# The order of the matmuls in a block product: the low half of the weights last

## The chip, the cores and the metric

The kernel runs on one core of a Trainium2 chip. The metric is the device time of one execution in microseconds (us), the median over several runs. Five engines matter. TensorE multiplies (PE in the profile; its loads of the stationary operand are the rows called PEld). VectorE (DVE) and ScalarE (ACT) do elementwise work, GpSimd (POOL) issues some transfers and a few elementwise operations, and SyncE (SP) issues the other transfers. Each engine takes its instructions in the order in which the program gives them, and waits where an operand is not ready yet.

## The reference, cut to what matters

The model is a two-layer encoder over 512 tokens of width 1024 (layer 0 mixes tokens by attention, layer 1 by a gated linear recurrence). Behind each mixer stands a multilayer perceptron, and only these two perceptrons are touched:

```python
D_MODEL, SEQ, DEPTH = 1024, 512, 2
D_FF = 4 * D_MODEL

def squared_relu_mlp(h, w1, w2):
    u = jax.nn.relu(h @ w1)
    return (u * u) @ w2

h = rms_norm(x, norm_mlp[layer])
x = x + squared_relu_mlp(h, mlp_w1[layer], mlp_w2[layer])
```

All of it is in 32-bit floats. The upward matrix `w1` is 1024 by 4096, the downward matrix `w2` 4096 by 1024.

## The kernel before, in words

**Halves.** The operands of these matmuls are tiles of the type fp32r. To keep the accuracy, each operand is split into a high half (the value cast to that type, names that end in `h`) and a low half (the rest, names that end in `l`), and a product is three matmuls: high by high, high by low, low by high. The split of a block of weights is two instructions of 128x1024 elements: ScalarE casts the raw block to `wh`, and then VectorE subtracts, `wl = raw - wh` (function `operand`). The activations are split in the same way, into `xgh`/`xgl` (the perceptron's input), and `bh`/`bl` and `sh`/`sl` (the squared hidden values).

**Quarters and block products.** The 4096 hidden features are worked through in four quarters (0 to 3). In each quarter the kernel computes hidden features from the input (the upward part) and multiplies them into the output (the downward part). Both parts use a scheme of Strassen's kind: seven block products, P1 to P7, on sums of blocks, take the place of eight. A quarter therefore has 14 upward steps (two halves p = 0 and 1 of the quarter, each in the order P1 P5 P6 P3 P7 P2 P4) and 14 downward steps. The downward steps are in a written order, `ORDERS["mid"]`: P1 0, P5 0, P1 1, P2 0, P5 1, P6 0, P6 1, P3 0, P3 1, P7 0, P7 1, P2 1, P4 0, P4 1, where the digit is the half g of the quarter. The last quarter of layer 1 has its own order, `"last"`, in which P2 1 stands behind P5 1. Quarter 0 has no upward steps here (plain products made it before). `run` lists all steps of a layer and goes through them; the last two downward steps of a layer (P4 0 and P4 1) are run by a function `end` and call `times`.

**An upward step** (`up`, matmuls on L976) is 24 matmuls of 256 columns: for two output halves i and four k, `wh` by h, `wl` by h, `wh` by l. The weights are the stationary operand. All 24 go into one bank of PSUM.

**A downward step** (`part` and `times`, matmuls on L1071) is 12 matmuls of 512 columns: for two token blocks i and two feature blocks j, h by `wh`, h by `wl`, l by `wh`. Here the activations are the stationary operand. Each i has a PSUM bank of its own. P1, P6, P7 and P4 go on adding to the same pair of banks (called X, `ps_t` in the trace), P5 and P3 to the pair V (`ps_acc`), P2 has the pair W (`ps_z`). Behind each step with g = 1, `collect` adds both banks to the output sums `c`, by one VectorE instruction a bank.

**What sets the order.** TensorE's order is the program's. Within a perceptron VectorE's and ScalarE's are too: the class `Ordered` chains each of their instructions behind the one before, so they all carry its line, L765. `leave(i)` issues what follows step i: copies out of PSUM, collects, and by `prepare(i + 4)` the additions of weight blocks, the split of hidden values that are still waiting (`split_slot`) and the split of the weights of the step four later (`make`, `operand`). There are four buffers for `wh` and four for `wl`, so the cast of step i + 4 takes the buffer of step i and cannot start before the last matmul that reads it. Transfers that add one block of weights to another in memory are issued from GpSimd (L1053).

Of the kernel before, what the change touches and what calls it, by code (L numbers as in the profile page):

```python
# [17 lines left out]
P = 128  # L18
S = 512
D = 1024  # L20
C = D // P
# [40 lines left out]
def hybrid_encoder(  # L62
# [24 lines left out]
    V, A, G, PE = nc.vector, nc.scalar, nc.gpsimd, nc.tensor  # L87
# [212 lines left out]
    with ExitStack() as actx:  # L300
# [12 lines left out]
        for i in range(2):  # L313
            both = []
            for nm in ("h", "l"):
                t = sp.tile([P, 2 * P], F32R, tag=f"last{nm}{i}", name=f"last{nm}{i}")
# [10 lines left out]
        q, kh, kl, v, w = {}, {}, {}, {}, {}  # L327
# [72 lines left out]
        sums = hp.tile([P, S], F32, tag="early", name="ssq")  # L400
# [4 lines left out]
        with tc.manual_schedule(engines=others):  # L405
# [26 lines left out]
            for k in range(C):  # L432
                for n, (low, y) in enumerate(((0, xgh), (0, xgl), (1, xgh))):
                    for i in range(2):
                        PE.matmul(
                            first[i], parts[i][low][:, k, :], y[:, k, :], start=k == n == 0,
                            stop=k == C - 1 and n == 2,
# [261 lines left out]
        steps = chain(*(g for g, _ in fill))  # L699
# [53 lines left out]
    HS = S // 2  # L753
# [21 lines left out]
    class Mlp:  # L775
# [191 lines left out]
        def up(self, name, w, ps, new):  # L967

            block = self.PRODUCTS[name][0]
            w = [t.rearrange("p j (k n) -> p (j k) n", n=2 * P) for t in w]  # L970
            for i in range(2):
                for k in range(C // 2):
                    h, l = self.xa(block, k)
                    wh, wl = (t[:, k, i * P : (i + 1) * P] for t in w)
                    for n, (m, y) in enumerate(((wh, h), (wl, h), (wh, l))):
                        PE.matmul(  # L976
                            ps[:, i * HS : (i + 1) * HS], m, y,
                            start=new and i == k == n == 0,
                            stop=i == 1 and k == C // 2 - 1 and n == 2,
                            skip_group_check=not new,  # L980
                        )

# [112 lines left out]
        def part(self, sums, name, g, w):  # L1097

            to = self.PRODUCTS[name][3]
            if to not in sums:  # L1100
                sums[to] = [self.bank() for _ in range(2)]
            for i in range(2):
                self.times(name, g, i, w, sums[to][i], name in ("P1", "P5", "P2"))

        OPEN_AT = 36
        UP = "P1", "P5", "P6", "P3", "P7", "P2", "P4"
# [297 lines left out]
    with ExitStack() as rctx:  # L1404
# [35 lines left out]
        ps, xc, aa, a0, om, z, gin, pg = ({} for _ in range(8))  # L1440
# [161 lines left out]
        for k in range(C):  # L1602
            for c in range(4):
                ps, wh, wl = begun[c]
# [196 lines left out]
```

## Time and profile before

| | |
|---|---|
| time, median of 3 runs | 1035.65 us (1035.09 to 1036.73) |
| the profiled execution's own time | 1035.46 us |
| its span | 1033.7 us |
| PE, PEld busy | 1023.5 us (99%), 890.9 us (86%) |
| DVE, ACT, POOL busy | 859.0 us (83%), 701.7 us (68%), 170.9 us (17%) |
| granted clock of TensorE | 0.999 |
| perceptron of layer 0, downward part of quarter 0 to the last step | about 290 to 563 us |
| perceptron of layer 1, the same | about 755 us to the end |

A row of the timeline gives the start in us from the beginning of the span, the duration in us, the engine, the line, the operation, output and inputs by the program's names, the shape, and in brackets the engine's idle time just before, with what ended it. Matmuls overlap one another and their ends are modelled, so the time that a matmul takes from the array is read from the distance between the starts of two of them, and not from its duration. A row of a group ends with the busy time, the mean of one in ns, and the idle time before the group's instructions.

### The profile page before, as it was taken

How to read it: one execution, taken by the hardware profiler on the slowest of the kernel's cores; microseconds unless marked ns; L12 is line 12 of the kernel's file. 1: busy time of each engine (PE TensorE's matmuls, PEld its weight loads, DVE VectorE, ACT ScalarE, POOL GpSimd, SP SyncE). 2: the span in 40 equal slices, each digit the busy share in tenths (PEclk: the TensorE clock that was granted, in tenths of full speed). 3: DMA queues.
4: the chain of work that ended last, by engine and by line, in shares of the span. 5: the costliest groups of instructions: out<-in, count | busy, mean ns of one | idle time of the engine just before them, and what ended most of it. 6: DMA issues, size and time to landing. Idle time of an engine off the chain costs nothing.

```text
span 1033.7 us, 15863 instructions
## 1 busy us (share of the span) xinstructions
PE 1023.5 (99%) x5862; PEld 890.9 (86%) x5862; DVE 859.0 (83%) x1148; ACT 701.7 (68%) x1083; POOL 170.9 (17%) x239
## 2 busy tenths in 40 slices
PE   9999999999999999999999999999999999999997
PEld 7888888888888988988988888888888988988986
DVE  6888787848788898898899888984789898898897
ACT  6777676836766873873875799964755773873866
POOL 0444344420010010010011121200010010010013
PEclk9999999999999999999999999999999999999999
DMA  7745354527536767667682575452436767667653
GB/s 241 212 121 144 114 151 103 159 97 288 145 77 190 183 139 201 172 139 200 173 207 79 153 185 151 103 223 83 101 66 182 180 146 194 171 145 198 165 117 111
DMA packets 53260, 160.46 MB, mean 155 GB/s; under 512 B 6720, under 2 KB 8256, under 8 KB 53184
## 3 DMA queue, kind: packets, MB, share of 16 engines
q1 hardware_dynamic: 42096, 120.35, 35.7%
q0 software_dynamic: 10656, 38.80, 22.6%
q8 instruction: 46, 0.75, 0.3%
q10 hardware_dynamic: 432, 0.31, 0.1%
q14 instruction: 30, 0.25, 0.1%
HBM read 137.41 MB, written 4.19 MB: 137 GB/s over the span
## 4 chain that ended last, share of the span: by engine, by line
PE 76%; DVE 12%; ACT 7%; issue 3%; DMA 1%; DVEq 0%; ACTq 0%; POOL 0%; POOLq 0%
PE ps_t L1071 10%; PE ps_acc L976 7%; DVE wl L765 5%; PE ps_acc L229 5%; PE ps_acc L231 5%; PE ps_acc L230 5%; PE ps_acc L1071 5%; PE ps_z L976 3%; ACT wh L765 3%; ACT u L765 3%; PE ps_t L229 2%; PE ps_z L1071 2%; PE ps_t L231 2%; PE ps_t L230 2%; DVE b L765 2%
## 5 line engine op out<-in xcount | busy, mean ns | idle before, releaser
L765 ACT CAST wh<-b 128x1024 fp32r<-128x1024 f32 x168 | 174.8, 1050 | 124.2 <-DVE b L765 79.2
L765 DVE TENSOR_TENSOR wl<-b,wh 128x1024 fp32r<-128x1024 f32 x168 | 203.5, 1219 | 43.3 <-ACT wh L765 42.8
L1053 POOL DMA_DIRECT2D b<-in_w_dn x40 | 35.0, 874 | 362.7 <-DVE b L765 268.3
L229 PE MATMUL ps_acc<-xgh,wh 128*128 128x512 f32 x192 | 78.5, 409 | 0.0
L231 PE MATMUL ps_acc<-xgl,wh 128*128 128x512 f32 x192 | 75.2, 392 | 0.0
L230 PE MATMUL ps_acc<-xgh,wl 128*128 128x512 f32 x192 | 75.1, 391 | 0.0
L224 DVE TENSOR_TENSOR wl<-raw,wh 128x512 fp32r<-128x512 f32 (+2 forms) x70 | 62.1, 914 | 14.5 <-ACT wh L222 14.3
L589 DVE TENSOR_TENSOR_SCAN scan<-keep,later 128x128 f32<-128x128 f32 (+1 forms) x64 | 59.5, 933 | 17.5 <-ACT keep L579 12.0
L765 ACT ACTIVATE u<-u 128x512 f32<-128x512 f32 x100 | 63.1, 632 | 9.8 <-DVE u L765 8.2
L222 ACT CAST wh<-raw 128x512 fp32r<-128x512 f32 (+2 forms) x70 | 50.7, 759 | 20.4 <-PE ps_acc L231 7.3
L593 POOL TENSOR_TENSOR w<-w,scan 128x128 f32<-128x128 f32 (+1 forms) x64 | 51.7, 810 | 58.4 <-DVE scan L589 56.4
L1053 POOL DMA_DIRECT2D b<-in_w_up x24 | 20.8, 868 | 236.6 <-DVE b L765 69.1
L765 DVE TENSOR_TENSOR b<-b,b 128x1024 f32<-128x1024 f32 x48 | 58.7, 1222 | 1.3
L765 DVE TENSOR_TENSOR u<-u 128x512 f32<-128x512 f32 (+1 forms) x92 | 54.8, 596 | 3.1 <-ACT u L765 1.1
L765 ACT CAST wh<-raw 128x1024 fp32r<-128x1024 f32 x46 | 48.1, 1048 | 8.4 <-PE ps_acc L1071 8.3
L976 PE MATMUL ps_z<-xgh,wh 128*128 128x256 f32 x192 | 53.1, 277 | 0.1
L976 PE MATMUL ps_z<-xgh,wl 128*128 128x256 f32 x192 | 53.0, 276 | 0.0
L976 PE MATMUL ps_acc<-low,wh 128*128 128x256 f32 x192 | 53.0, 276 | 0.0
L1071 PE MATMUL ps_t<-wl,sh 128*128 128x512 f32 x126 | 49.7, 395 | 1.1 <-DVE wl L765 1.1
L1071 PE MATMUL ps_t<-wh,sl 128*128 128x512 f32 x126 | 49.7, 394 | 0.0
L1071 PE MATMUL ps_t<-wh,bh 128*128 128x512 f32 x126 | 49.2, 390 | 0.0
L1071 PE MATMUL ps_t<-wh,sh 128*128 128x512 f32 x126 | 49.1, 390 | 0.0
(399 smaller groups left out, 3408.7 us busy)
## 6 DMA issues: line engine op xcount, KB each, us to landing
b<-in_w_dn SPq DMA_DIRECT2D x48, 512.0 KB, 4.4
b<-in_w_dn POOLq DMA_DIRECT2D x40, 512.0 KB, 5.7
b<-in_w_up SPq DMA_DIRECT2D x36, 512.0 KB, 4.8
b<-in_w_up POOLq DMA_DIRECT2D x24, 512.0 KB, 5.6
raw<-in_w_m SPq DMA_DIRECT2D x16, 512.0 KB, 4.5
raw<-in_w_dn SPq DMA_DIRECT2D x16, 512.0 KB, 4.6
raw<-in_w_in SPq DMA_DIRECT2D x16, 512.0 KB, 3.8
raw<-in_w_qk SPq DMA_DIRECT2D x12, 512.0 KB, 3.7
```

What stands on the lines that cost most here:

```text
L222: A.copy(wh[:, k, :], raw[:, k, :])
L224: V.tensor_tensor(wl[:, k, :], raw[:, k, :], f(wh[:, k, :]), ALU.subtract)
L229: PE.matmul(ps, wh, ah, start=start, stop=False)
L230: PE.matmul(ps, wl, ah, start=False, stop=False)
L231: PE.matmul(ps, wh, al, start=False, stop=stop)
L589: V.tensor_tensor_scan(sc[:, S - n : S][:, ::-1], keep[:, :n][:, ::-1], later[:, S - n :][:, ::-1], 1.0, ALU.mult, ALU.max,)
L593: G.tensor_tensor(wt, wt, sc[:, S - n + 1 : S + 1], ALU.mult)
L765: ins = getattr(self.e, name)(*args, **kwargs)
L976: PE.matmul(ps[:, i * HS : (i + 1) * HS], m, y, start=new and i == k == n == 0, stop=i == 1 and k == C // 2 - 1 and n == 2, skip_group_che ...
L1053: G.dma_start(out=unit[b].rearrange("p j n -> p (j n)"), in_=unit["src"](to), accum_op=ALU.add)
L1071: PE.matmul(ps, m, y[:, jj, cols], start=first and n == 0, stop=last and n == 2, skip_group_check=not new,)
```

## The change

The order of the matmuls within a step changes, in the upward and in the downward steps. Neither their number nor their operands change. In an upward step, first come the 16 matmuls with `wh` (h and l by turns, through both i and all k), and then the eight with `wl`. In a downward step, first come the eight with `wh` (h and l by turns, through i and j), and then the four with `wl`. The flags that open and close the sums in PSUM move to the first and the last matmul of the new order. `part` now has the loop itself; `times` is left as it was, for `end`.

```diff
 # up
-            for i in range(2):
-                for k in range(C // 2):
-                    h, l = self.xa(block, k)
-                    wh, wl = (t[:, k, i * P : (i + 1) * P] for t in w)
-                    for n, (m, y) in enumerate(((wh, h), (wl, h), (wh, l))):
-                        PE.matmul(
-                            ps[:, i * HS : (i + 1) * HS], m, y,
-                            start=new and i == k == n == 0,
-                            stop=i == 1 and k == C // 2 - 1 and n == 2,
-                            skip_group_check=not new,
-                        )
+            steps = [(low, i, k) for low in range(2) for i in range(2) for k in range(C // 2)]
+            for low, i, k in steps:
+                h, l = self.xa(block, k)
+                wh, wl = (t[:, k, i * P : (i + 1) * P] for t in w)
+                for m, y in ((wl, h),) if low else ((wh, h), (wh, l)):
+                    PE.matmul(
+                        ps[:, i * HS : (i + 1) * HS], m, y,
+                        start=new and i == k == low == 0 and y is h,
+                        stop=(low, i, k) == steps[-1], skip_group_check=not new,
+                    )
 # part
-            for i in range(2):
-                self.times(name, g, i, w, sums[to][i], name in ("P1", "P5", "P2"))
+            block, new = self.PRODUCTS[name][0], name in ("P1", "P5", "P2")
+            wh, wl = w
+            steps = [(low, i, j) for low in range(2) for i in range(2) for j in range(2)]
+            for low, i, j in steps:
+                h, l = (t[:, j, block, i * P : (i + 1) * P] for t in self.a[g])
+                for m, y in ((h, wl),) if low else ((h, wh), (l, wh)):
+                    PE.matmul(
+                        sums[to][i], m, y[:, j, :],
+                        start=new and g == j == low == 0 and m is h,
+                        stop=g == low == j == 1, skip_group_check=not new,
+                    )
```

## The prediction

> **What bounds the kernel now.** I read the page first, then the groups of PE and PEld by shape, then the timeline of PE alone in one downward part, and then VectorE's and ScalarE's rows beside it.
>
> ```profile
> PE 1023.5 (99%) x5862; PEld 890.9 (86%) x5862; DVE 859.0 (83%) x1148; ACT 701.7 (68%) x1083; POOL 170.9 (17%) x239
> L1071 PEld LDWEIGHTS ps_t<-wl,sh 128*128 128x128 f32 x126 | 23.6, 188 | 8.3 <-DVE wl L765 3.5
> ```
>
> PE is the bound, and by its 99% it seems to have nothing to give. The second row says otherwise: loads that go with a matmul on `wl` wait for VectorE. The modelled ends hide it, so I take starts. This is the downward part of layer 0, quarter 2: the first matmuls of P1 1, P2 0, P5 1, P6 0, P6 1 (with its second and third) and P3 0.
>
> ```profile
> 450.04 0.39 PE L1071 MATMUL ps_t<-wh,sh 128*128 128x512 f32 x1
> ...
> 452.87 0.39 PE L1071 MATMUL ps_z<-wh,bh 128*128 128x512 f32 x1
> ...
> 455.83 0.39 PE L1071 MATMUL ps_acc<-wh,sh 128*128 128x512 f32 x1
> ...
> 458.81 0.39 PE L1071 MATMUL ps_t<-wh,bh 128*128 128x512 f32 x1
> ...
> 461.53 0.39 PE L1071 MATMUL ps_t<-wh,sh 128*128 128x512 f32 x1
> 462.13 0.50 PE L1071 MATMUL ps_t<-wl,sh 128*128 128x512 f32 x1 [0.21 <-DVE wl L765]
> 462.47 0.40 PE L1071 MATMUL ps_t<-wh,sl 128*128 128x512 f32 x1
> ...
> 464.80 0.39 PE L1071 MATMUL ps_acc<-wh,bh 128*128 128x512 f32 x1
> ```
>
> ```profile
> 449.73 0.69 DVE L765 TENSOR_TENSOR sl<-u,sh 128x512 fp32r<-128x512 f32 x1
> 460.85 1.23 DVE L765 TENSOR_TENSOR wl<-b,wh 128x1024 fp32r<-128x1024 f32 x1 [0.57 <-ACT wh L765]
> 463.13 0.74 DVE L765 SCALAR_TENSOR_TENSOR c<-ps_acc,rr,c 128x512 f32<-128x512 f32 x1
> ```
>
> A step without a wait, P6 0, takes 461.53 - 458.81 = 2.72 us, 0.227 a matmul. P2 0 takes 2.96, P5 1 2.98 and P6 1 3.27: 0.24, 0.26 and 0.55 lost, 1.05 a quarter. In P6 1 the cause can be read. The second matmul should start at 461.53 + 0.227 = 461.76, but VectorE ends `wl` at 460.85 + 1.23 = 462.08. It starts 0.05 later, at 462.13, and the third comes 0.34 behind it in place of 0.227: a late operand costs its lateness, plus 0.05, plus 0.11 for the load that could not be made ahead, 0.165 together. P1 1 loses 0.11 in another way: `sl` ends at 449.73 + 0.69 = 450.42, while the third matmul, the first to read it, is due at 450.04 + 2 x 0.227 = 450.49; less than 0.165 ahead, so about 0.1 is lost.
>
> The Trainium skill ("TensorE: Matmul & The Clock Gate", "Step-by-step: what each phase is for") says that TensorE pulls weight loads ahead of running matmuls. In a downward product the load is of h and not of `wl`, so by that rule nothing but the 0.05 would follow a late `wl`, and the bounds below, which hold 0.165, would each move by 0.115; five of them would add 0.6 us to the gain, an estimate. The trace does not bear it out here: the load's own row waits for `wl`, and the third matmul came 0.34 behind.
>
> **The change part by part.** The count of instructions on every queue stays; only PE's order moves, and with it when operands fall due and when buffers and banks come free.
>
> *`wl` falls due later.* Downward it is first read by matmul 9 in place of 2, 7 x 0.227 = 1.59 us later. The lateness in the rows was at most 462.08 - 461.76 = 0.32, and all the time won since P1 1 (under 1 us) still fits in 1.59. So these waits go. What is late next? P3 0 adds to the bank V, which VectorE must have collected. Its first collect of V ends at 463.13 + 0.74 = 463.87, so P3 0 can start at 463.87 + 0.165 = 464.04 at the earliest: a bound of 464.80 - 464.04 = 0.765 on the quarter's gain while VectorE keeps its times. VectorE and ScalarE hardly wait for PE in this stretch, so they do keep them. The other full quarters, P1 1, VectorE's collect, P3 0 each (layer 0 quarters 1 and 3, layer 1 quarters 1 and 2):
>
> ```profile
> 372.53 0.39 PE L1071 MATMUL ps_t<-wh,sh 128*128 128x512 f32 x1
> 385.68 0.74 DVE L765 SCALAR_TENSOR_TENSOR c<-ps_acc,rr,c 128x512 f32<-128x512 f32 x1
> 387.30 0.39 PE L1071 MATMUL ps_acc<-wh,bh 128*128 128x512 f32 x1
> ...
> 527.54 0.39 PE L1071 MATMUL ps_t<-wh,sh 128*128 128x512 f32 x1
> 540.63 0.74 DVE L765 SCALAR_TENSOR_TENSOR c<-ps_acc,rr,c 128x512 f32<-128x512 f32 x1
> 542.27 0.39 PE L1071 MATMUL ps_acc<-wh,bh 128*128 128x512 f32 x1
> ...
> 838.45 0.39 PE L1071 MATMUL ps_t<-wh,sh 128*128 128x512 f32 x1
> 851.72 0.74 DVE L765 SCALAR_TENSOR_TENSOR c<-ps_acc,rr,c 128x512 f32<-128x512 f32 x1
> 853.36 0.39 PE L1071 MATMUL ps_acc<-wh,bh 128*128 128x512 f32 x1
> ...
> 916.10 0.39 PE L1071 MATMUL ps_t<-wh,sh 128*128 128x512 f32 x1
> 929.19 0.74 DVE L765 SCALAR_TENSOR_TENSOR c<-ps_acc,rr,c 128x512 f32<-128x512 f32 x1
> 930.81 0.39 PE L1071 MATMUL ps_acc<-wh,bh 128*128 128x512 f32 x1
> ```
>
> From P1 1 to P3 0 stand five steps, 13.60 us without waits. Lost are 14.77 - 13.60 = 1.17, 1.13, 1.31 and 1.11 (1.16 in the quarter above). The bounds by V are 387.30 - 386.585 = 0.715, 0.735, 0.735 and 0.715.
>
> *The low halves of the activations fall due one matmul earlier*, 0.227 us downward. In P1 1 `sl` is late already, so its wait grows by that: above, from 0.1 to 450.42 + 0.165 - 450.27 = 0.315. Then 1.16 - 0.315 = 0.845 could be won, still over the bound of 0.765; in the other four quarters, by the same step, about 0.8 each, also over it. So V decides, and the sum of the five is 0.715 + 0.765 + 0.735 + 0.735 + 0.715 = 3.67.
>
> *`wh` comes free earlier.* Upward its last read is matmul 16 of 24 in place of the last, 8 x 0.113 = 0.9 us (half of 0.227 each, for half the columns). ScalarE's casts that wait for the buffer start earlier:
>
> ```profile
> 417.57 1.05 ACT L765 CAST wh<-b 128x1024 fp32r<-128x1024 f32 x1 [1.19 <-PE ps_acc L976]
> 418.66 1.23 DVE L765 TENSOR_TENSOR wl<-b,wh 128x1024 fp32r<-128x1024 f32 x1 [0.39 <-ACT wh L765]
> 420.29 0.59 ACT L765 COPY u<-ps_acc 128x512 f32<-128x512 f32 x1 [0.47 <-PE ps_acc L976]
> 421.18 1.05 ACT L765 CAST wh<-b 128x1024 fp32r<-128x1024 f32 x1 [0.29 <-DVE b L765]
> ```
>
> The cast at 417.57 waited for PE. If it goes 0.9 earlier, VectorE's `wl` at 418.66 gains its idle 0.39, and the next cast, which waited for VectorE, gains 0.3, up to the end of the copy at 420.88. From there I followed VectorE's and ScalarE's rows to `sl` at 449.73 and the collect at 463.13, and no wait on PE cuts the 0.3 off. So in such a quarter `sl` comes 0.3 earlier, its wait nearly vanishes (450.12 + 0.165 against 450.27), and the bound by V rises by 0.3. The same wait stands in layer 0 quarter 3 and layer 1 quarter 2; in layer 0 quarter 1 a transfer holds VectorE back and I take 0.05, in layer 1 quarter 1 nothing. No row shows the cast going early, so the ends are 0 and 0.95 in all, and I take 0.95, since the row names PE as what it waited for.
>
> *Quarter 0 of layer 0*, P2 0 to P5 1:
>
> ```profile
> 298.59 0.39 PE L1071 MATMUL ps_z<-wh,bh 128*128 128x512 f32 x1
> 301.63 0.39 PE L1071 MATMUL ps_acc<-wh,sh 128*128 128x512 f32 x1
> ```
>
> 3.04 - 2.72 = 0.32 is won, with no `sl` late. The same step in layer 1 I count at nothing, because PE waits for ScalarE and VectorE soon after. There the early low halves cost something too:
>
> ```profile
> 796.75 0.28 PE L976 MATMUL ps_acc<-s,wh 128*128 128x256 f32 x1
> 797.15 0.69 DVE L765 TENSOR_TENSOR low<-x,s 128x512 fp32r<-128x512 f32 x1
> ...
> 818.88 0.39 PE L976 MATMUL ps_z<-bh,wh 128*128 128x256 f32 x1 [0.20 <-ACT u L765]
> ```
>
> The step at 796.75 reads the last `low` (done at 797.84) with matmul 8 in place of 12, due at 796.75 + 7 x 0.113 = 797.54: 0.46 late with the 0.165. The wait at 818.88 takes up part of it; I charge 0.2, between 0 and 0.46.
>
> *The first of two banks closes later.* Downward the bank of i = 0 is complete after matmul 10 in place of 6. In most places VectorE collects it long after, or PE needs it a step later. Not at the end of layer 1, where P4 0 adds to X right behind P7 1 (P1 1 of that quarter, P7 0, P7 1, and two collects of X):
>
> ```profile
> 993.55 0.39 PE L1071 MATMUL ps_t<-wh,sh 128*128 128x512 f32 x1
> 1016.13 0.39 PE L1071 MATMUL ps_t<-wh,bh 128*128 128x512 f32 x1
> 1018.85 0.39 PE L1071 MATMUL ps_t<-wh,sh 128*128 128x512 f32 x1
> 1020.54 0.74 DVE L765 SCALAR_TENSOR_TENSOR c<-ps_t,rr,c 128x512 f32<-128x512 f32 x1
> 1021.78 0.75 DVE L765 SCALAR_TENSOR_TENSOR c<-ps_t,rr,c 128x512 f32<-128x512 f32 x1 [0.43 <-PE ps_t L1071]
> ```
>
> Eight steps from 993.55 to 1016.13 take 22.58 in place of 21.76, so 0.82 is lost and PE may reach P7 1 0.8 earlier, at 1018.05. Its tenth matmul starts at 1018.05 + 9 x 0.227 = 1020.09; VectorE starts 0.43 behind a last matmul (1021.78 against P7 1's last at 1018.85 + 11 x 0.227 = 1021.35), so at 1020.52, is done at 1021.26, and P4 0 starts at 1021.43 in place of 1018.85 + 2.72 = 1021.57. Of 0.8 won 0.15 is left; without the 0.3 on `sl` it is -0.15.
>
> *Sum:* 3.67 + 0.95 + 0.32 - 0.2 + 0.15 = 4.9 us. Against the profiled execution's 1035.46 (its span of 1033.7 and 1.8 around it) that is 1030.6; it stands 0.2 below the median of 1035.65, and so I predict 1030.8 for the median. Steps without a late `wl` keep 2.72.
>
> **The rivals.**
> 1. *The buffers' part does not come.* ScalarE's early cast may be held by something behind PE. Then 3.67 + 0.32 - 0.2 - 0.15 = 3.6 us: 1032.0. For it: I saw no such cast go early. Against it: PE is named in the row.
> 2. *VectorE gives it all back.* If PE's lead runs into VectorE in each quarter, behind the V bound too (the collects of X before P7 0), the time ends where it was, about 1035. For it: V already leaves under 1 us. Against it: behind P3 0 the steps have no wait in the rows, and P7 0 comes two steps later.
> 3. *Slower, by the collects.* Each downward step with g = 1 hands over its first bank 4 x 0.227 = 0.9 us later; a collect that waits holds the low halves queued behind it on VectorE. At the end of such a step both collects end 0.25 later than now (first bank at matmul 10 plus 0.43, then two of 0.7). With seven such steps in each of eight quarters, all on the path, it is 56 x 0.25 = 14 us; with the three at each quarter's end, where VectorE has caught up, 24 x 0.25 = 6 us against 3.6 won: 1038. It decides from the point at which a `wl` has less than 0.25 left when it falls due. Against it: it now falls due 1.59 later.
> 4. *More than I count.* Every loss between the heads goes, 1.17 + 1.16 + 1.13 + 1.31 + 1.11 + 0.82 + 0.32 = 7.0 us: 1028.6. It needs the bank V collected earlier than its rows say.
>
> **How the numbers follow.** Forecast 0.50, rival 1 0.25, rival 2 0.10, rival 3 0.10, rival 4 0.05. Rivals 1 and 4 are faster too: 0.80 faster, 0.10 the same, 0.10 slower, with 0.2% (2.1 us) as about what a measurement of this kernel can tell from no change. The range reaches from 1029.2, between the forecast and rival 4, past rival 1 to 1034.2, and leaves out rival 3 and most of rival 2.
>
> **What would show it.** In the profile after, P2 0, P5 1 and P6 1 take 2.72, and waits on `wl` leave PE's list. P3 0's first matmul stands within 0.2 of the end of V's first collect. The cast that stood at 417.57 starts about 0.9 ahead of the end of its step. P4 0 of the last quarter waits for `c`. P1 1 shows whether `sl` came 0.3 earlier (no loss) or not (0.3). The prediction is wrong if upward steps change their 2.72, or a wait on `sl` or on a bank takes up what `wl` gave.

## The result and the profile after

The changed kernel takes 1031.24 us (median of 6 runs, 1030.67 to 1031.54). The kernel before, beside it on the same chip, takes 1036.31 us (6 runs, 1035.09 to 1038.13). The ratio is 0.9949, with a 95% interval of 0.9938 to 0.996: faster by 0.5%. The prediction was 1030.8 us, with a range of 1029.2 to 1034.2. The profiled execution took 1031.54 us, with a span of 1029.5 us.

The page of the kernel after, its busy times and two groups of matmuls (output, inputs, count, busy us, mean ns, then the idle time and what ended most of it):

```profile
PE 1018.6 (99%) x5862; PEld 892.2 (87%) x5862; DVE 857.8 (83%) x1148; ACT 700.9 (68%) x1083; POOL 172.6 (17%) x239
...
L1107 PE MATMUL ps_t<-wh,sl 128*128 128x512 f32 x120 | 47.0, 391 | 0.4 <-DVE sl L765 0.2
L976 PE MATMUL ps_acc<-low,wh 128*128 128x256 f32 x192 | 44.9, 277 | 0.5 <-DVE low L765 0.5
```

PE is at 99% as before, although 4.9 us of its busy time have gone: that share said nothing of the waits. The Trainium skill warns of this ("Perfetto Trace Analysis", "Identifying the Most-Contended Engine": the busy time of matmuls is a poor measure of how near a kernel is to its limit, because they are pipelined), and this pair of pages agrees with it. The waits that remain on the matmuls' operands are named `sl` and `low`, the low halves of the activations. `wl`, to which 3.5 us of the loads' idle time were put before in the group shown there alone, is not among them any more.

The same stretch as in the prediction, layer 0, quarter 2, in the timeline of the kernel after (start, duration, engine, line, operation): PE's first matmuls of P1 1, P2 0, P5 1, P6 0, P6 1, P3 0 and P3 1, and then rows of VectorE.

```profile
449.51 0.39 PE L1107 MATMUL ps_t<-wh,sh 128*128 128x512 f32 x1
...
452.26 0.39 PE L1107 MATMUL ps_z<-wh,bh 128*128 128x512 f32 x1
...
454.98 0.39 PE L1107 MATMUL ps_acc<-wh,sh 128*128 128x512 f32 x1
...
457.70 0.39 PE L1107 MATMUL ps_t<-wh,bh 128*128 128x512 f32 x1
...
460.42 0.39 PE L1107 MATMUL ps_t<-wh,sh 128*128 128x512 f32 x1
...
463.14 0.41 PE L1107 MATMUL ps_acc<-wh,bh 128*128 128x512 f32 x1
...
465.92 0.39 PE L1107 MATMUL ps_acc<-wh,sh 128*128 128x512 f32 x1
```

```profile
448.80 0.68 DVE L765 TENSOR_TENSOR sl<-u,sh 128x512 fp32r<-128x512 f32 x1
...
462.20 0.74 DVE L765 SCALAR_TENSOR_TENSOR c<-ps_acc,rr,c 128x512 f32<-128x512 f32 x1
```

P2 0, P5 1, P6 0 and P6 1 all take 2.72 us now, where the first, second and fourth took 2.96, 2.98 and 3.27. From P1 1 to P3 0 it is 463.14 - 449.51 = 13.63 in place of 14.76: 1.13 of the 1.16 us that were lost are won. P3 0 has just reached the next bound: VectorE ends the first collect of V at 462.20 + 0.74 = 462.94, P3 0 starts 0.20 behind that, and takes 465.92 - 463.14 = 2.78, 0.06 over 2.72.

Below, the gain is followed as a lead. The lead of a kernel at some step is the time from its first downward step to that step in the kernel before, minus the same in this kernel, each from one profiled execution. The work ahead of that first step is left out, because it is the same and varies by itself (it ends between 289.3 and 292.0 us in the executions profiled here). The first step in the kernel before and in the kernel after:

```profile
290.43 0.39 PE L1071 MATMUL ps_t<-wh,bh 128*128 128x512 f32 x1
```

```profile
290.81 0.39 PE L1107 MATMUL ps_t<-wh,bh 128*128 128x512 f32 x1
```

At P1 1 of this quarter the lead is (450.04 - 290.43) - (449.51 - 290.81) = 0.91 us, and at the end of the span (1033.7 - 290.43) - (1029.5 - 290.81) = 4.6. The spans differ by only 4.2, because the first step came 0.38 later in the second execution. The same measure part by part, beside the terms of the prediction:

| part | predicted | lead won |
|---|---|---|
| layer 0, quarter 0 | 0.32 | 0.32 |
| layer 0, quarter 1 | 0.715 + 0.05 | 0.59 |
| layer 0, quarter 2 | 0.765 + 0.3 | 1.08 |
| layer 0, quarter 3 | 0.735 + 0.3 | 1.00 |
| layer 1, quarter 0 | 0 | 0.28 |
| layer 1, upward part of quarter 1 | -0.2 | -0.43 |
| layer 1, downward part of quarter 1 | 0.735 | 0.63 |
| layer 1, quarter 2 | 0.715 + 0.3 | 1.04 |
| layer 1, quarter 3 to the end | 0.15 | 0.10 |
| sum | 4.9 | 4.6 |

### The profile page after: what moved, and what is told of

Its sections match the earlier page's. It is cut to its first block, busy times and chain, and to the rows that moved or that the text cites. A ratio compares the mean times of both kernels' runs of the same rounds, so it can differ in the third digit from the quotient of the medians.

```text
span 1029.5 us, 15878 instructions
## 1 busy us (share of the span) xinstructions
PE 1018.6 (99%) x5862; PEld 892.2 (87%) x5862; DVE 857.8 (83%) x1148; ACT 700.9 (68%) x1083; POOL 172.6 (17%) x239
## 4 chain that ended last, share of the span: by engine, by line
PE 87%; DVE 6%; ACT 3%; issue 2%; DMA 1%; POOL 0%; SPq 0%; DVEq 0%; ACTq 0%; POOLq 0%
PE ps_t L1107 13%; PE ps_acc L1107 8%; PE ps_acc L976 7%; PE ps_z L976 5%; PE ps_acc L229 5%; PE ps_acc L231 5%; PE ps_acc L230 5%; PE ps_z L1107 4%; PE ps_o L976 3%; DVE wl L765 2%; PE ps_t L229 2%; PE ps_t L231 2%; PE ps_t L230 2%; PE ps_o L229 2%; PE ps_o L231 2%; PE ps_o L230 2%
## 5 line engine op out<-in xcount | busy, mean ns | idle before, releaser
L1107 PE MATMUL ps_t<-wh,sl 128*128 128x512 f32 x120 | 47.0, 391 | 0.4 <-DVE sl L765 0.2
L1107 PE MATMUL ps_t<-wh,bh 128*128 128x512 f32 x120 | 46.8, 390 | 0.0
L1107 PE MATMUL ps_t<-wh,bl 128*128 128x512 f32 x120 | 46.8, 390 | 0.0
L1107 PE MATMUL ps_t<-wh,sh 128*128 128x512 f32 x120 | 46.7, 390 | 0.0
L765 DVE TENSOR_TENSOR sl<-u,sh 128x512 fp32r<-128x512 f32 (+2 forms) x50 | 37.4, 749 | 10.3 <-ACT sh L765 10.3
L976 PE MATMUL ps_acc<-low,wh 128*128 128x256 f32 x192 | 44.9, 277 | 0.5 <-DVE low L765 0.5
L765 DVE TENSOR_TENSOR wl<-raw,wh 128x1024 fp32r<-128x1024 f32 x36 | 44.3, 1229 | 0.8 <-ACT wh L765 0.8
```

What stands on the lines that cost most here:

```text
L765: ins = getattr(self.e, name)(*args, **kwargs)
L976: PE.matmul(ps[:, i * HS : (i + 1) * HS], m, y, start=new and i == k == low == 0 and y is h, stop=(low, i, k) == steps[-1], skip_group_che ...
L1107: PE.matmul(sums[to][i], m, y[:, j, :], start=new and g == j == low == 0 and m is h, stop=g == low == j == 1, skip_group_check=not new,)
```

## The experiments

The table gives each run's median, that of the kernel before on the same chip, the ratio, and the lead at five places: the last step of layer 0, the first upward step of layer 1, the first downward step of its quarter 1, the first upward step of its quarter 3, and the end. The changed kernel stands there three times; the last column says whether the upward steps of layer 1, quarter 1 ran at 2.72 or 2.83 us a step (see the last section).

| kernel | us | before | ratio (95%) | lead at the five places | step |
|---|---|---|---|---|---|
| changed | 1031.24 | 1036.31 | 0.9949 (0.9938 to 0.996) | 2.99, 3.27, 2.84, 4.51, 4.61 | 2.72 |
| upward alone | 1034.56 | 1035.59 | 0.9992 (0.9983 to 1.0001) | 0.75, 0.77, -0.21, 0.72, 1.09 | 2.83 |
| downward alone | 1032.53 | 1035.59 | 0.9966 (0.9954 to 0.9979) | 2.33, 2.63, 2.49, 3.77, 3.54 | 2.72 |
| three passes | 1031.68 | 1035.59 | 0.9963 (0.995 to 0.9975) | 2.76, 2.90, 2.81, 4.18, 4.39 | 2.72 |
| by bank | 1030.99 | 1035.59 | 0.9952 (0.9939 to 0.9966) | 3.32, 3.59, 2.37, 4.53, 4.89 | 2.83 |
| upward alone, `wl` first | 1035.79 | 1035.44 | 1.0001 (0.9991 to 1.001) | -0.03, -0.03, 0.00, 0.01, -0.04 | 2.72 |
| downward alone, `wl` first | 1038.01 | 1035.44 | 1.0025 (1.0014 to 1.0035) | -0.81, -1.03, -1.08, -1.53, -2.70 | 2.72 |
| by bank, three passes | 1030.89 | 1035.44 | 0.9953 (0.994 to 0.9965) | 3.08, 3.39, 3.15, 4.81, 5.19 | 2.72 |
| changed, second time | 1030.93 | 1035.44 | 0.9956 (0.9943 to 0.9968) | 3.16, 3.47, 1.76, 3.41, 3.52 | 2.83 |
| changed, collects swapped | 1036.01 | 1035.77 | 0.9997 (0.9988 to 1.0006) | 0.68, 0.29, -0.27, 0.57, -0.76 | 2.83 |
| before, collects swapped | 1037.82 | 1035.77 | 1.0016 (1.0007 to 1.0025) | -0.28, -0.67, -0.35, -0.42, -2.14 | 2.72 |
| pairs | 1030.94 | 1035.77 | 0.995 (0.9937 to 0.9962) | 2.99, 3.27, 3.09, 4.76, 5.12 | 2.72 |
| changed, third time | 1031.02 | 1035.77 | 0.9953 (0.9939 to 0.9966) | 3.15, 3.41, 2.99, 4.62, 4.71 | 2.72 |

### The two halves of the change alone

The upward steps alone are changed (the first hunk of the change), or the downward steps alone (the second).

```diff
 # e1_up_only: up
-                    for n, (m, y) in enumerate(((wh, h), (wl, h), (wh, l))):
...
+            steps = [(low, i, k) for low in range(2) for i in range(2) for k in range(C // 2)]
```

> Only the upward steps have the new order; the downward steps are those of before. My theory: the cast of a later wh starts 0.9 us earlier, VectorE's chain behind it 0.3 us earlier in layer 0 quarters 2 and 3 and layer 1 quarters 2 and 3, so that the waits of the downward part, which are VectorE's, shrink by 0.3 us a quarter: 4 x 0.3 = 1.2 won, less 0.2 for the low halves that fall due earlier in the first upward part of layer 1: about 1.0 us faster than before, with P6 1 still over 3.0 us long. The rival, that the earlier free buffers play no part and the gain is the later due wl alone: nothing won, 0.2 us slower than before.

```diff
 # e2_down_only: part
-                self.times(name, g, i, w, sums[to][i], name in ("P1", "P5", "P2"))
...
+            steps = [(low, i, j) for low in range(2) for i in range(2) for j in range(2)]
```

> Only the downward steps have the new order; the upward steps are those of before. My theory: the waits on wl go, VectorE's times stay, and PE's lead in a full quarter is bounded by the collect of the bank V ahead of P3 0, about 0.7 us in each of five quarters, with a wait of about 0.3 us on sl in P1 1 in all of them: 3.6 + 0.3 for the first quarter - 0.15 at the end, about 3.6 us faster than before. With the upward steps alone it adds up to the whole change (1.0 + 3.6 against 4.6 in the trace). The rival, without a part of the buffers: this kernel alone gives the whole 4.6 us or more, and P1 1 takes as long as in the changed kernel.

The upward half won 1.09 us of lead and 1034.56 against 1035.59 in the medians, whose interval just takes in no change (0.9983 to 1.0001), so its gain rests on the trace. The downward half won 3.54 and 1032.53 against 1035.59. In layer 0 the two add up: 0.75 + 2.33 = 3.08, where the three profiles of the changed kernel have 2.99 to 3.16. That they do so at the end too, 4.63 against 4.61, is in part luck. In layer 1's first upward part the trace of the upward half ran at the slower pace and lost 0.98 of lead, the changed kernel 0.43; from there to the end the halves won 1.30 and 1.05, the whole change 1.77. The prediction's 0.95 for the buffers of `wh`, for which no row had been there, is the upward half: it won 0.43, 0.39 and 0.39 in the three quarters for which 0.3 each was predicted. The rival that this part does not come has fallen.

### The low half first, upward

The same rearrangement of an upward step with the two passes exchanged: the eight matmuls with `wl` first, the 16 with `wh` behind them. Then `wh` is read up to the last matmul, as before, and `wl` sooner than before. If the upward gain came from the order as such, it should stay; if it came from the buffer of `wh`, it should go.

```diff
 # up
-            steps = [(low, i, k) for low in range(2) for i in range(2) for k in range(C // 2)]
+            steps = [(low, i, k) for low in (1, 0) for i in range(2) for k in range(C // 2)]
```

> Only the upward steps are changed, and the other way round: the eight matmuls with wl come first, then the sixteen with wh, so that wh is read up to the last matmul as before the change and wl is due at once; the downward steps are those of before. My theory, that the gain of the upward part is the buffer of wh that comes free 0.9 us earlier: the 0.3 us a quarter that the upward order alone gave are not there, the leads at the ends of the quarters stay within 0.1 us of before, and no step waits for wl, since it was ready 0.6 us and more ahead. The rival, that any order that sorts the upward matmuls by weights gives the gain: about 1.0 us, as in the run with the upward order alone.

Nothing is left of it: 1035.79 against 1035.44, and the lead stays within 0.04 of zero. ScalarE's rows show why. A copy out of PSUM and, behind it, the cast that the prediction named (of the kernel before only the copy, since its cast at 417.57 stands above); before, after, and in the kernel with `wl` first:

```profile
414.85 0.59 ACT L765 COPY u<-ps_acc 128x512 f32<-128x512 f32 x1 [0.24 <-PE ps_acc L976]
```

```profile
414.32 0.59 ACT L765 COPY u<-ps_acc 128x512 f32<-128x512 f32 x1 [0.24 <-PE ps_acc L976]
...
416.14 1.05 ACT L765 CAST wh<-b 128x1024 fp32r<-128x1024 f32 x1 [0.28 <-PE ps_acc L976]
```

```profile
414.76 0.59 ACT L765 COPY u<-ps_acc 128x512 f32<-128x512 f32 x1 [0.23 <-PE ps_acc L976]
...
417.48 1.05 ACT L765 CAST wh<-b 128x1024 fp32r<-128x1024 f32 x1 [1.19 <-PE ps_acc L976]
```

From the copy to the cast it is 417.57 - 414.85 = 2.72 us before, 1.82 after and 2.72 with `wl` first: a whole step of PE, or a step less the 0.9 us of the eight matmuls that no longer stand ahead of the last one with `wh`. The cast still waits for PE in the kernel after, but 0.28 us in place of 1.19.

### The low half first, downward

The downward step alone, with its four matmuls with `wl` first. Two theories of the downward gain are told apart: that the alternation of `wl` and `wh` cost something by itself (then this order wins too), or that the lateness of `wl` did (then it loses, because four matmuls stand at the head where `wl` is wanted at once).

```diff
 # part
-            steps = [(low, i, j) for low in range(2) for i in range(2) for j in range(2)]
+            steps = [(low, i, j) for low in (1, 0) for i in range(2) for j in range(2)]
```

> Only the downward steps are changed, and the other way round: the four matmuls with wl come first, then the eight with wh. wl is due one matmul (0.227 us) earlier than before the change, the low halves of the activations three matmuls later. My theory, that VectorE's wl sets the end of P6 1 (of P2 0 in the first quarters, of P3 1 in the last): each of eight quarters loses about 0.23 us more, 1.6 to 2.0 us slower than before, and P1 1 loses nothing on sl, which does not help because the next wl is VectorE's. The rival, that what was lost was a cost of alternating wh and wl and not lateness: faster than before by a good part of the changed kernel's gain.

It is slower: 1038.01 against 1035.44, ratio 1.0025, and the lead is -2.70 at the end. P6 1 of layer 0, quarter 2 (the last matmul of P6 0, the first two of P6 1; the second row groups two):

```profile
461.72 0.39 PE L1108 MATMUL ps_t<-wh,bl 128*128 128x512 f32 x1
462.37 0.73 PE L1108 MATMUL ps_t<-wl,sh 128*128 128x512 f32 x2 [0.26 <-DVE wl L765]
```

The first matmul of P6 1 now waits for `wl`: it starts 0.65 behind the one before it in place of 0.227. It is the lateness that counts. The size was expected at 1.6 to 2.0: at P7 1 of the last quarter the lead is -1.78, as expected, and another 0.92 goes behind that step, which was not expected and whose cause is open.

### Which bound comes next: the collect of V

The prediction said that V's first collect is next behind `wl`, 0.715 to 0.765 away, which is about the 0.74 of one collect. So the two collects behind each step with g = 1 are exchanged, in both kernels: bank 1 is collected first, and bank 0, which P3 0 needs first, one collect later. In the kernel before there is just enough room for that; in the changed kernel, if V is its bound, there is none.

```diff
 # leave
-                        for n in range(2):
+                        for n in (1, 0):
```

> The kernel before the change with the same edit, collects the other way round. In its trace the second collect of V ends 0.1 us ahead of where P3 0 would have to wait for it. My theory: the full quarters lose 0 to 0.1 us each, and the end loses 1.5 to 1.8 us at P4 0, which adds to X right behind P7 1. The rival, that the order of the collects costs the same whatever the order of the matmuls: P3 0 is 0.6 us later in each of five quarters here too, 3 us and the end.

> The changed kernel with one edit: the two collects behind a downward step are issued the other way round, the second bank first. Nothing is left out. The collect that P3 0 waits for first then lands one collect, about 0.7 us, later, and the other one earlier. My theory, that the collect of the bank V bounds the lead in five quarters: P3 0 starts 0.6 to 0.7 us later in each, 3.0 to 3.5 us, and the last P4 0, which waits for a collect of X already, loses 1.0 to 1.3 more: about 4 us slower than the changed kernel, almost all its gain. The rival, that P3 0's short wait in the changed kernel is no bound: the quarters keep their leads and only the end loses, 1.0 to 1.3 us.

Before, the swap cost 1037.82 against 1035.77, and 1.75 of the 2.14 us of lost lead came at P4 0 of the last quarter, where PE needs X at once. Up to the end of layer 0 it cost 0.28. The changed kernel lost all of its gain: 1036.01 against 1035.77, where the changed kernel itself took 1031.02 in the same series. That is 5.0 us slower, more than the 4 expected. P6 1 and P3 0 of layer 0, quarter 2 with the swap, and VectorE's two collects of V in one row; the changed kernel and then the one before:

```profile
460.88 0.39 PE L1107 MATMUL ps_t<-wh,sh 128*128 128x512 f32 x1
...
464.04 0.47 PE L1107 MATMUL ps_acc<-wh,bh 128*128 128x512 f32 x1 [0.28 <-DVE c L765]
464.34 0.39 PE L1107 MATMUL ps_acc<-wh,bl 128*128 128x512 f32 x1
```

```profile
462.49 1.41 DVE L765 SCALAR_TENSOR_TENSOR c<-ps_acc,rr,c 128x512 f32<-128x512 f32 x2
```

```profile
465.43 0.39 PE L1071 MATMUL ps_acc<-wh,bh 128*128 128x512 f32 x1
```

```profile
463.80 1.40 DVE L765 SCALAR_TENSOR_TENSOR c<-ps_acc,rr,c 128x512 f32<-128x512 f32 x2
```

In the changed kernel the second collect ends at 462.49 + 1.41 = 463.90, P3 0 starts 0.14 behind it, and P6 1 takes 464.04 - 460.88 = 3.16 in place of 2.72: PE waits for the bank and nothing else. In the kernel before the second collect ends at 465.20, and P3 0 starts at 465.43 without a wait. So V was not in the way before, with a slack of one collect, and it is the bound now.

Not all of what the changed kernel lost by the swap was lost at V. A full quarter of layer 0 won 0.35 to 0.40 with the swap where it won 1.0 to 1.1 without (quarters 2 and 3), and about 0.20 of that difference went two steps ahead of P3 0, at P6 0, which adds to X. The collects of X and the first matmul of P6 0, in the changed kernel with the swap:

```profile
456.49 1.41 DVE L765 SCALAR_TENSOR_TENSOR c<-ps_t,rr,c 128x512 f32<-128x512 f32 x2
```

```profile
458.04 0.47 PE L1107 MATMUL ps_t<-wh,bh 128*128 128x512 f32 x1
```

P6 0 starts 0.14 behind the end of the second collect at 457.90; P5 1 takes 2.80 there and P6 0 2.84. So in the changed kernel X has less than one collect of slack as well.

### Other orders of the same matmuls

Four orders were tried for a version that beats the change, against the waits that the trace after still shows. In the first, each step is three passes (high by high, low activation by `wh`, high by `wl`), so that `sl` and `low` fall due later.

```diff
 # up
+            steps = [(n, i, k) for n in range(3) for i in range(2) for k in range(C // 2)]
...
 # part
+            steps = [(n, i, j) for n in range(3) for i in range(2) for j in range(2)]
...
+                m, y = ((h, wh), (l, wh), (h, wl))[n]
```

> In both kinds of step three passes: all matmuls of high by high, then those with the low half of the activations, then those with the low half of the weights. The low halves of the activations fall due later (matmul 5 of 12, matmul 9 of 24), the rest is as in the changed kernel. My theory: the waits on sl in P1 1 (0.41 and 0.49 us in quarter 1 of the two layers) and on low in the first upward part of layer 1 (0.73) go, but the first two come back one for one as a longer wait of P3 0 for the collect of V, and a part of the third before P6 of the same part: 0.2 to 0.5 us faster than the changed kernel. The rival, that nothing of VectorE bounds PE behind P1 1: all of it is won, 1.6 us faster than the changed kernel, and P3 0 keeps 2.72 to 2.84 us.

That was missed: 1031.68, with a lead of 4.39, a little less than the change. The wait on `sl` did go, but the second bank is now wanted by matmul 3 of a step and not by matmul 5. P3 0 of layer 0, quarter 2, its first three matmuls (each row groups two: the one named by its start, and the one behind it), and VectorE's collect of the second bank:

```profile
464.23 0.68 PE L1107 MATMUL ps_acc<-wh,bh 128*128 128x512 f32 x2
464.52 0.76 PE L1107 MATMUL ps_acc<-wh,bh 128*128 128x512 f32 x2
464.78 0.73 PE L1107 MATMUL ps_acc<-wh,bh 128*128 128x512 f32 x2
```

```profile
463.98 0.74 DVE L765 SCALAR_TENSOR_TENSOR c<-ps_acc,rr,c 128x512 f32<-128x512 f32 x1
```

The second collect ends at 464.72 and the third matmul starts 0.06 behind it; P3 0 takes 2.93 us here, and 2.96, 2.96, 2.97 and 2.97 in the other four full quarters, against 2.76 to 2.84 after the change. V takes back what `sl` gave. The fourth matmul comes late once more, 465.12 - 464.78 = 0.34 behind the third in place of 0.227, to which the last section returns.

In the second, a downward step goes bank by bank: for i = 0 the four with `wh` and the two with `wl`, then the same for i = 1. The upward steps are those of the change.

```diff
 # part
-            steps = [(low, i, j) for low in range(2) for i in range(2) for j in range(2)]
+            steps = [(low, i, j) for i in range(2) for low in range(2) for j in range(2)]
```

> The downward steps go bank by bank: for each of the two token blocks the four matmuls with wh and then its two with wl; the upward steps as in the changed kernel. The first bank closes with matmul 6 of 12 as before the change, and wl falls due at matmul 5 in place of 9. My theory: the wait of 0.7 us before the last product P4 0 of layer 1 goes (0.64 + 0.08 in the changed kernel's trace), the 0.17 around P4 0 of layer 1's first quarter may go, P6 1 waits for wl by about 0.1, and the bound by V stays: 0.4 to 0.8 us faster than the changed kernel. The rival, that the late first bank holds VectorE up in all quarters: over 1.5 us faster. The other rival, that four matmuls are too little for wl: waits of 0.2 us and more a quarter come back, and it is slower than the changed kernel.

1030.99 and a lead of 4.89, 0.28 more than the change and less than the 0.4 to 0.8 expected. The first bank closes at matmul 6 again, and the last quarter shows it: P4 0 waits 0.28 us for X there, after the change 0.64. In layer 1's first upward part this trace lost 3.59 - 2.37 = 1.22 us of lead at the slower pace, against 3.27 - 2.84 = 0.43 after, but in the downward part behind it it won 1.15, against 0.63 after. So the order may be worth some 0.3 more than its lead says; the medians can't tell.

The third joins both: bank by bank, three passes within a bank, and the upward steps in three passes.

```diff
 # part
+            steps = [(n, i, j) for i in range(2) for n in range(3) for j in range(2)]
```

> Downward bank by bank as in the run that did so, and within a bank high by high twice, then the low half of the activations twice, then the low half of the weights twice; upward in three passes. Due are: sl at matmul 3 of 12 as before the change, wl at 5, low at matmul 9 of 24; the first bank closes with matmul 6. My theory: the gains of the bank-by-bank run (4.9 in its trace) stay, the wait for low in the first upward part of layer 1 shrinks from 0.7 to 0.2 and the slower steps behind it go (about 0.9), P1 1 loses 0.2 less in two quarters: 5.5 to 6.2 us faster than before, 0.8 to 1.5 faster than the changed kernel. The rival, that VectorE's collects take it back as in the run with three passes: 4.4 to 5.0 us faster than before.

Missed as well: 1030.89, a lead of 5.19. `wl` falls due at matmul 5, and in the first full quarter of each layer that is too soon. P6 1 of layer 1, quarter 1 (a row groups two) and VectorE's two `wl` ahead of the collects, in one row:

```profile
845.80 0.63 PE L1107 MATMUL ps_t<-wh,sh 128*128 128x512 f32 x2
846.26 0.61 PE L1107 MATMUL ps_t<-wh,sl 128*128 128x512 f32 x2
846.86 0.73 PE L1107 MATMUL ps_t<-wl,sh 128*128 128x512 f32 x2
```

```profile
845.58 2.36 DVE L765 TENSOR_TENSOR wl<-b,wh 128x1024 fp32r<-128x1024 f32 x2 [0.57 <-ACT wh L765]
```

The fifth matmul should start at 845.80 + 4 x 0.227 = 846.71 and starts at 846.86, and the one behind it loses another 0.11; the step takes 3.01.

The fourth puts the four matmuls with `wl` behind all others again, keeps two passes bank by bank ahead of them and three passes upward, and goes bank by bank only in P7 1 of the last quarter.

```diff
 # part
+            if by_bank:
+                steps = [(n, i, j) for i in range(2) for n in range(3) for j in range(2)]
+            else:
+                steps = [(n, i, j) for i in range(2) for n in range(2) for j in range(2)]
+                steps += [(2, i, j) for i in range(2) for j in range(2)]
```

> A version put together from the runs so far: upward in three passes; downward, for each token block high by high twice and low half of the activations twice, then at the end the four matmuls with wl; P7 1 of the last quarter of layer 1 alone goes bank by bank. Due are: sl at matmul 3, the second bank of V at matmul 5, wl at matmul 9, low at matmul 9 of 24. My theory: P6 1 no longer waits for wl as it did bank by bank (0.23 in quarter 1 of both layers), P3 0 is bounded as in the changed kernel, the wait for low is 0.1 to 0.3 and no slow upward steps follow it, and the last P4 0 waits 0.3 in place of 0.7: 5.2 to 5.7 us faster than before, 0.6 to 1.0 faster than the changed kernel where its upward steps keep 2.72 us. The rival, that what is left is bounded by VectorE altogether: no faster than bank by bank with passes, 5.2.

1030.94 and a lead of 5.12, just under the 5.2 to 5.7 expected. P2 0 and P5 1 take 2.72 in every quarter, but in the first full quarter of a layer P3 0 waits 0.28 and 0.24 us for V, with what was won ahead of it. So three orders reach a lead of 4.9 to 5.2, and their medians of 1030.89 to 1030.99 can't be told from the 1031.02 and 1030.93 of the change beside two of them. No order of the matmuls was found that measurably beats it.

### The changed kernel again

The change as it is, without an edit, in two later series.

> The changed kernel once more, beside the others on the same chip: 4.5 to 5.1 us faster than before, with the same waits in the downward parts. What is open is the pace of the upward steps in layer 1 quarter 1 behind the wait for low: 2.72 us a step as in its first trace, or 2.83 as in two of the other runs; if it can be either from run to run, the time scatters by about 1.2 us.

> The changed kernel a third time, for a comparison with the version above on one chip, and for the pace of the upward steps behind the wait for low in layer 1 quarter 1: 2.72 us a step as in its first trace (4.6 us won in all) or 2.83 as in its second (3.5 won in all).

Medians 1030.93 and 1031.02; their traces have leads of 3.52 and 4.71. The difference lies in one place, layer 1's first upward part, and is told in the last section.

## Why the prediction was right, point by point

**`wl` due later: as predicted.** P2 0, P5 1 and P6 1 take 2.72 in every quarter (P6 1 up to 2.77), and `wl` has left PE's waits. That it was the lateness is shown by the order with `wl` first. The estimate that the prediction worked out from the rule of the Trainium skill ("TensorE: Matmul & The Clock Gate", "Step-by-step: what each phase is for"), by which only 0.05 would follow a late operand, stays unsupported: behind each late low half that is left, the matmul next to the one that waited comes 0.11 late once more (below).

**V's first collect as the next bound: as predicted**, and shown by the swapped collects. What the prediction took too low is the price of running into it. It put P3 0's start at 0.165 behind the end of the collect, and the step at 2.72. P3 0 of layer 0, quarter 1 in the kernel after (its first two matmuls) and the collect:

```profile
386.67 0.47 PE L1107 MATMUL ps_acc<-wh,bh 128*128 128x512 f32 x1
386.97 0.39 PE L1107 MATMUL ps_acc<-wh,bl 128*128 128x512 f32 x1
```

```profile
385.77 0.74 DVE L765 SCALAR_TENSOR_TENSOR c<-ps_acc,rr,c 128x512 f32<-128x512 f32 x1
```

The start is 0.16 behind 386.51, as said, but the second matmul then comes 0.30 behind the first in place of 0.227, and the step takes 2.82: the late bank costs 0.16 + 0.10 = 0.26 together, not 0.165. P3 0 took 2.82, 2.78, 2.82, 2.84 and 2.76 in the five full quarters, 0.42 us in all over 2.72. That term was left out. It is more than the whole shortfall of 4.9 against 4.6, because other terms came out better than predicted.

**`wh` free earlier: as predicted in mechanism, the size too small.** The cast goes 0.9 earlier, but VectorE's work behind it comes 0.40 earlier and not 0.3. In layer 0, quarter 2, it is 463.13 - 450.04 = 13.09 us from P1 1 to V's first collect before and 462.20 - 449.51 = 12.69 after, and the same in layer 0, quarter 3, and layer 1, quarter 2. The prediction let the next cast start at the end of the copy ahead of it; in the kernel after it starts 0.49 behind the start of the copy (419.76 and 420.25), 0.10 ahead of the end of the copy's row. That these three quarters won 1.08, 1.00 and 1.04, against 1.065, 1.035 and 1.015 predicted, is therefore in part luck: the 0.1 too little here and the price of V left out above cancel. Where 0.05 was taken, in layer 0, quarter 1, it was less than nothing in this profile: the distance was 385.68 - 372.53 = 13.15 before and is 13.18 now. The second and third profile of the changed kernel have 12.99 and 13.08 there and won 0.77 and 0.71 in that quarter in place of 0.59, so this part differs from execution to execution.

**The low halves due earlier: right where VectorE ran ahead, and decisive where it did not.** In quarter 1 of layer 0 `sl` got no advance, and P1 1 lost what the prediction's sum gives for that case. Its first three matmuls and `sl`:

```profile
372.59 0.39 PE L1107 MATMUL ps_t<-wh,sh 128*128 128x512 f32 x1
373.12 0.50 PE L1107 MATMUL ps_t<-wh,sl 128*128 128x512 f32 x1
373.46 0.40 PE L1107 MATMUL ps_t<-wh,sh 128*128 128x512 f32 x1
```

```profile
372.38 0.68 DVE L765 TENSOR_TENSOR sl<-u,sh 128x512 fp32r<-128x512 f32 x1
```

`sl` ends at 373.06, the second matmul starts 0.06 later and 0.30 late, and the third 0.34 behind it: 0.41 in all. The other four steps gave it back, up to the bound by V.

**Layer 1, quarter 0: counted at nothing, won 0.28.** P2 0's 0.32 and P6 1's 0.11 were won, and 0.16 went at P4 0, two steps behind P7 1, which waits for VectorE's collect of X. That wait was not foreseen: the prediction looked at this bank in the last quarter only, and told of it elsewhere in a rival. P4 0, and the collect of X's first bank:

```profile
785.44 0.47 PE L1107 MATMUL ps_t<-wh,bh 128*128 128x512 f32 x1
```

```profile
784.55 0.74 DVE L765 SCALAR_TENSOR_TENSOR c<-ps_t,rr,c 128x512 f32<-128x512 f32 x1
```

The collect ends at 785.29, and P4 0 starts 0.15 behind it.

**`low` due earlier: the direction was right, the size too small.** The step with its seventh, eighth and ninth matmuls and the last `low`:

```profile
793.87 0.28 PE L976 MATMUL ps_acc<-s,wh 128*128 128x256 f32 x1
...
794.55 0.28 PE L976 MATMUL ps_acc<-s,wh 128*128 128x256 f32 x1
795.29 0.39 PE L976 MATMUL ps_acc<-low,wh 128*128 128x256 f32 x1 [0.46 <-DVE low L765]
795.51 0.28 PE L976 MATMUL ps_acc<-s,wh 128*128 128x256 f32 x1
...
797.34 0.28 PE L976 MATMUL ps_acc<-bh,wh 128*128 128x256 f32 x1
```

```profile
794.54 0.69 DVE L765 TENSOR_TENSOR low<-x,s 128x512 fp32r<-128x512 f32 x1
```

The eighth matmul should follow the seventh at 794.55 + 0.113 = 794.66, and starts at 795.29, 0.06 behind the end of `low` and 0.63 late; the ninth is 0.11 later still. The step takes 797.34 - 793.87 = 3.47, 0.75 over 2.72, where 0.46 was computed. The 0.28 won in quarter 0, with which it had not been credited, brought PE that much nearer to VectorE. 0.33 of it came back in the second half of the part, so -0.43 is left. With quarter 0 the two make -0.15, against -0.2 predicted: one error paid for the other.

**The end: as predicted.** P7 1's first matmul and P4 0's, and VectorE's collect of X:

```profile
1013.92 0.39 PE L1107 MATMUL ps_t<-wh,sh 128*128 128x512 f32 x1
...
1017.28 0.47 PE L1070 MATMUL ps_t<-wh,bh 128*128 128x512 f32 x1 [0.48 <-DVE rt L1677]
```

```profile
1016.38 0.75 DVE L765 SCALAR_TENSOR_TENSOR c<-ps_t,rr,c 128x512 f32<-128x512 f32 x1 [0.28 <-PE ps_t L1107]
```

The tenth matmul is at 1013.92 + 9 x 0.227 = 1015.96, the collect starts 0.42 behind it (0.43 was taken) and ends at 1017.13, and P4 0 starts 0.15 later. The lead falls from 5.32 to 4.68 there; 0.10 is left of the 0.8 won, where 0.15 was predicted. The row names `rt` as what P4 0 waited for, a small instruction that ends beside the collect; that the bank is meant is argued from the distance, 0.15 behind the collect as at P3 0, and from the order that closes this bank earlier, in which the wait shrank to 0.28.

**The rivals.** The first (buffers' part does not come) fell by the upward half alone and by the casts' rows. The second and third (VectorE gives it back, or the collects cost more) did not decide, though the places they named are where the shortfall lies. The fourth (more than counted) needed V earlier than its rows, and V held.

## What to carry to other kernels

Within a group of matmuls that go on adding to the same bank, the operand that is made last should be read last: it costs no instruction, and here it was worth three quarters of the gain. The operand whose buffer the next producer waits for should be read first and let go, which was worth the rest. Then look for what is late next before counting the gain: here a bank that VectorE must empty stood 0.75 us behind the wait that went, and the orders that ran into it sooner gave back there what they won elsewhere.

## What the hardware showed that was not expected

**Two paces of the same matmuls.** Behind the wait on `low` the stream of 256-column matmuls can go on at one of two paces, with the same operands, line and granted clock of TensorE (0.998 to 0.999). The first matmuls of two upward steps behind that wait, in the kernel after and in the same kernel's second profile:

```profile
797.34 0.28 PE L976 MATMUL ps_acc<-bh,wh 128*128 128x256 f32 x1
...
800.06 0.28 PE L976 MATMUL ps_acc<-s,wh 128*128 128x256 f32 x1
```

```profile
795.70 0.28 PE L976 MATMUL ps_acc<-bh,wh 128*128 128x256 f32 x1
...
798.53 0.28 PE L976 MATMUL ps_acc<-s,wh 128*128 128x256 f32 x1
```

A step takes 2.72 us in the first and 2.83 in the second, 113.3 and 117.8 ns a matmul. The slower pace held for six steps, to the next wait; in the traces of the upward half alone, of the order by bank, and of the changed kernel with its collects swapped it held for all 12 steps that were left of the part. In the others, the first and third profile of the changed kernel among them, the steps right behind that wait ran at 113 ns, but for a few matmuls. The slower pace is not bound to the wait on `low`, though. The first profile of the changed kernel has it in two later steps of the same part (P6 and P3 of p = 1). The kernel before with its collects swapped has it in three steps of layer 0's first upward part (P7, P2 and P4 of p = 1). And the first upward step of each quarter that has upward steps takes 2.87 us in every run, 119.5 ns a matmul, with no wait in it: in the kernel before, layer 0, quarter 2, it starts at 406.34 and the step behind it at 409.21.

Over layer 1's first upward part the second profile lost 1.71 us of lead (3.47 to 1.76), the first 0.43: the difference is more than any other order added to the change. The Trainium skill ("TensorE: Matmul & The Clock Gate", "Back-to-back issue gap") gives the distance of two matmuls as the columns over 2.4 GHz plus about 2.5 ns, 109 ns for 256 columns, for isolated matmuls; both paces are above that. What sets the pace is open: the wait on `low` led to the one and to the other, and the slower one is there without it.

**What a late bank costs.** A first matmul of a step that waits for a bank starts 0.14 to 0.16 behind the end of the collect, and the next one comes about 0.08 late (P3 0 above; P4 0 at 785.44 and at 1017.28 start the same 0.15 behind). For `sl` and `low` it was 0.06 and 0.11. The difference does not lie in the bank as such: in the order in three passes the third matmul of P3 0 waits for the second bank, starts 464.78 - 464.72 = 0.06 behind the collect, and the fourth comes 0.11 late, just as with a late operand. What the traces show besides is a separate semaphore instruction of 0.05 us in PE's queue, ahead of each first matmul that started 0.15 behind a collect (at 386.56 for P3 0 above, where the collect ends at 386.51), and none ahead of the waits of 0.06. That it makes the difference is likely and not shown: no run leaves it out.
